# A decoder layer on one core: the attention branch's product for the prompt alone, weight splits in program order, and another order of the cache tiles

## The chip, the cores and the metric

One core of one Trainium2 chip runs the whole kernel. The metric is the device time in microseconds, the median of several runs; lower is better.

## What is computed

One decoder layer with shared weights for two groups of tokens: a prompt of 512 tokens and 32 sampled tokens (8 sequences of 4, each with 4096 past tokens in a paged cache). D is 1024, there are 8 heads of 64, everything is fp32. Cut to what matters here:

```
h  = rms_norm(x) * (1 + sc_m) + sh_m
u, q, k, v, g_a, g_b = split(h @ w_in)
a  = pool_mixer(u) @ w_branch_pool
o  = attend(q, k, v) @ w_branch_attn        # prompt: block-sparse; sampled: over the cache
m  = sigmoid(g_a) * a + sigmoid(g_b) * o
x  = x + gt_m * (m @ w_out)
h2 = rms_norm(x) * (1 + sc_f) + sh_f
x  = x + gt_f * ((silu(conv3(h2 @ w_up_gate)) * (h2 @ w_up_val)) @ w_down)
```

The six vectors sh_m, sc_m, gt_m, sh_f, sc_f, gt_f (modulations 0 to 5) are products of the tokens' conditions with w_ada.

## The kernel before

**Layout.** The 544 columns (512 of the prompt, then 32 sampled) lie feature-major and are worked in two halves of 272 columns (`BOTH`, `HALF`). A product in fp32 is made of three fp32r products, `mm3` (line 458): weight hi by input hi, hi by lo, lo by hi. So every weight tile is split in two on chip: ScalarE copies it to `hi` (line 182) and VectorE subtracts to get `lo` (line 179); `split` (line 184) writes both.

**Weights.** `granule_plan` (line 54) lists the 512 KB granules in the order of use: q, k, v, u, then ga, ga, bp four times (gate a and the pool branch), gb eight times, ba four times (the attention branch), wo eight times, then the feed-forward part: 44 granules ahead of the latter. `W.pump` (line 214) loads them on SP's queue into a ring of three staging tiles `st` (some at the start in pairs, `pair`). `W.get` (line 239) hands out a split granule and has the next one split at once (`conv`, line 225), into rings of two `hi` and two `lo`; wo's granules get tiles of their own (`woh`, `wol`). A scheduler of the framework then sets each engine's order of instructions from its own estimates, so a split may stand elsewhere in ScalarE's or VectorE's order than where it is written, unless it is pinned. `pin` (`keep_in_program_order`) ties an instruction behind the instruction written before it on its engine.

**Two streams.** `dense1` (line 483) is the dense work up to wo. `kv_stream` (line 1006) works the paged cache for the sampled tokens: 64 key tiles of 1 MB (products `qk`), two softmaxes of 4 sequences each (`soft`, line 1054), 64 value tiles (`pv`, 8 per sequence), and the modulations 2 to 5 from w_ada (`mod`, `one`). Its tiles come on POOL's queue into a ring of six buffers `kv`, in the order of `kv_order` (line 1335): 32 key tiles, 4 more, 32 value tiles, the other 28 key tiles, modulations 4 and 5 (4 tiles each), 32 value tiles, modulations 2 and 3 (8 tiles). PE takes them in visits of four tiles (`RUN`) which a loop (after line 1297) puts between pieces of `dense1` by its own estimate of PE's clock and of each tile's landing; a stream can also wait for a named state (`need`). PE, ScalarE and VectorE each work their instructions in the resulting order.

**The end of the two streams.** After the last gate product `dense1` waits for `oTs` (line 900), the sampled attention of all eight sequences; `finish` (line 1012) makes it: it masks a sequence's `pv` result, and its `rest` transposes it (`oT`) ahead of the next visit and reduces it into `oTs`. Then come the O products (line 907 on, two halves of 272 columns), the split of the merged m (`mh`, `ml`), the need for modulations 2 and 4, and wo (line 977 on): eight products over the first half of the columns, eight over the second. After each, `residual` (line 940) adds x (loaded again from `xT`) and ScalarE squares the sum (`sq`).

Of the kernel before, what the change touches and what calls it, by code (L numbers as in the profile page):

```python
# [73 lines left out]
def body(ctx, tc, I, O):  # L74
# [46 lines left out]
    V, A = nc.vector, nc.scalar  # L121

# [82 lines left out]
    class Weights:  # L205
# [19 lines left out]
        def conv(self, i):  # L225
            if i >= len(self.jobs) or self.jobs[i][1] or i in self.done:
                return
            self.pump()
            st = self.tiles.pop(i)
            if i in self.hooks:  # L230
                self.hooks.pop(i)(st)
            hi, lo = self.place.pop(i)() if i in self.place else (wsh.next(), wsl.next())
            split(hi, lo, st)
            self.done[i] = (hi, lo)
            self.ready[i] = max(PE.now, self.landed.pop(i)) + SPLIT_US
            self.held -= 1
            self.pump()
# [26 lines left out]
    csT = consts.tile([128, KD, 32], F32, name="csT")  # L264
# [4 lines left out]
    cst = consts.tile([128, NCONST], F32, name="cst")  # L269
    par = consts.tile([128, NPAR], F32, name="par")  # L270
# [4 lines left out]
    ones = consts.tile([128, 1], F32, name="ones")  # L275
    V.memset(ones, 1.0)

    pin = tc.keep_in_program_order
# [40 lines left out]
    class Stream:  # L319
# [7 lines left out]
        def pump(self):  # L327
            while self.issued < len(self.items) and self.issued < self.at + NKV:
# [32 lines left out]
                self.landed[self.issued] = Q.move(1.0, POOL_US.get(kind, 1.0))  # L361
# [25 lines left out]
    modT = consts.tile([128, 6, 8, 9], F32, name="modT")  # L387
# [95 lines left out]
    def dense1():  # L483
# [90 lines left out]
        def heads_sampled(name, got):  # L574
# [4 lines left out]
            if name == "q":  # L579

                qa = consts.tile([128, 4, 2, 32], F32, name="qall")
# [12 lines left out]
            else:  # L594
                hs = consts.tile([128, 4, NS], F32, name=name + "sT")
# [155 lines left out]
        def weigh(i, f):  # L751
# [8 lines left out]
            if i == 3:  # L760
                of = slot([128, T])
                act(of[:, 0:S], o)
                attn.append(of)
# [88 lines left out]
        Tt = []  # L852
        def gate(f, sig):
# [8 lines left out]
        for f0 in range(0, 8, 2):  # L862
# [6 lines left out]
            for f in (f0, f0 + 1):  # L869
                yield from gate(f, sig_a)  # L870
                if f == 0:
# [4 lines left out]
            for f in (f0, f0 + 1):  # L876
# [10 lines left out]
        sg = {}  # L887

        def sig_b(f, ps):
            sg[f] = slot([128, T])  # L890
            for o, (a, b) in zip(ps, BOTH):
                act(sg[f][:, a:b], o, AF.Sigmoid)
        for f in range(8):
            yield from gate(f, sig_b)
        ohl = []
        for of in attn:
            oh, ol = slot([128, T], F32R), slot([128, T], F32R)
            split(oh[:, 0:S], ol[:, 0:S], of[:, 0:S])
# [5 lines left out]
        yield ("lat", 2.0)  # L904
        for f0 in range(0, 8, 2):
            ba = W.get()
# [9 lines left out]
        ohl.clear()  # L916


        mh, ml = [slot([128, T], F32R) for _ in range(8)], [slot([128, T], F32R) for _ in range(8)]
        for f in range(8):  # L920
            split(mh[f], ml[f], Tt[f])
# [53 lines left out]
        for a, b in BOTH:  # L975
            pr, sq = mm([128, HALF], "ss"), []
# [29 lines left out]
    def kv_stream():  # L1006
        fin, Ls, PTs, own_p, stats, pvs = [], {0: [], 1: []}, {}, {}, {}, {}
# [4 lines left out]
        def finish(n, pv):  # L1012
# [4 lines left out]
            def rest():  # L1017
# [4 lines left out]
                if n == NSEQ - 1:  # L1022
                    state["oTs"] = True
            fin.append(rest)

        def kstep(g, c):
# [13 lines left out]
            if c % 4 == 3:  # L1040
# [6 lines left out]
                Ls[g].append(l)  # L1047
            if c == NPG - 1:
# [92 lines left out]


# [8 lines left out]
        while todo:  # L1151
            kind, a = todo[0]
            if kind == "done":
# [4 lines left out]
            while n < min(RUN, len(todo)) and todo[n][0] in ("k", "v", "m"):  # L1158
                if todo[n][0] == "v":
                    yield ("need", "PT%d" % (todo[n][1][0] // 4))  # L1160
                    yield ("need", "vs")
# [3 lines left out]
            while fin:  # L1165
                fin.pop(0)()
                yield ("x", 0.45)
# [12 lines left out]
            PE.end()  # L1180
            del todo[:n]
# [153 lines left out]
def kv_order():  # L1335
# [3 lines left out]
    return k[0] + k[1][:4] + v[:32] + k[1][4:] + [("one", 4), ("one", 5)] + v[32:] + [("mod", 1)]  # L1339
# [129 lines left out]
```

## Time and profile before

| what | value |
|---|---|
| runs | 981.67, 982.39, 984.0 us; median 982.39 |
| profiled execution | 982.47 us, its span 980.7 us, granted TensorE clock 0.982 of full speed |
| busy, share of the span | PE 95%, VectorE 48%, ScalarE 33%, POOL 14% |
| moved | 231.77 MB: 151.00 MB on POOL's queue, 79.48 MB on SP's |

PE is TensorE's matmuls; DVE is VectorE, ACT is ScalarE. Matmuls are pipelined and their ends are modelled, so a row's own duration is not its cost: the cost of one in a row of equal products is the distance between starts. In the profile each value tile shows eight `pv` records (in the order listings below, four products). Rows in square brackets give the idle time before an instruction and what ended it.

### The profile page before, as it was taken

The numbers are of one execution on the slowest core, as the hardware profiler recorded it, in microseconds if no ns is written. First come the engines' busy times: TensorE is split into PE (matmuls) and PEld (weight loads), VectorE is DVE, ScalarE is ACT, GpSimd is POOL, SyncE is SP. The second block draws the span as 40 slices with busy tenths as digits, with TensorE's granted clock in tenths as the row PEclk, the third lists the DMA queues.
The fourth block names the chain that finished last, engine by engine and source line by source line (L and its number), as shares of the span: only waits on it lengthen the run. The fifth ranks groups of instructions, "written<-read, shape, count | busy, mean of one in ns | idle before, by whom it ended". The sixth has DMA issues, their size and how long they took to land.

```text
span 980.7 us, 20374 instructions
## 1 busy us (share of the span) xinstructions
PE 931.1 (95%) x8724; PEld 807.0 (82%) x8724; DVE 475.1 (48%) x1155; ACT 323.3 (33%) x645; POOL 138.1 (14%) x153
## 2 busy tenths in 40 slices
PE   4999998799899999998699999999999999999998
PEld 2567776555589998874279999999999999999998
DVE  5673526766413234222157656554454546444643
ACT  4352426633312226312034544332322323123210
POOL 0133333033423322334200000000000000000000
PEclk9999999999999999999799999999999999999999
DMA  9799999399989999899976102222222222222332
GB/s 359 271 397 415 402 422 378 146 358 370 367 335 415 399 416 402 342 420 418 422 290 222 64 1 87 88 89 89 98 91 87 86 87 86 87 87 87 94 98 81
DMA packets 45354, 231.77 MB, mean 236 GB/s; under 512 B 5136, under 2 KB 6672, under 8 KB 25808
## 3 DMA queue, kind: packets, MB, share of 16 engines
q0 software_dynamic: 20736, 151.00, 38.0%
q1 hardware_dynamic: 24528, 79.48, 23.1%
q8 instruction: 68, 1.11, 0.5%
q14 instruction: 22, 0.18, 0.1%
HBM read 225.52 MB, written 4.94 MB: 235 GB/s over the span
## 4 chain that ended last, share of the span: by engine, by line
PE 82%; DVE 8%; DMA 4%; ACT 3%; issue 2%; POOL 0%; ACTq 0%; POOLq 0%; DVEq 0%
PE up L162 26%; PE dn L162 13%; PE gate L162 10%; PE qkv L162 7%; PE qk L162 5%; PE pv L162 5%; PE wo L162 4%; PE A L162 3%; DMA kv<-in_v,vidx 3%; PE mod L162 2%; DVE s L179 2%; ACT s L182 2%; PE paO L162 1%; PE paS L162 1%; DMA st<-in_wpack 1%
## 5 line engine op out<-in xcount | busy, mean ns | idle before, releaser
L162 PE MATMUL up<-s,hi 128*128 128x272 f32 x1408 | 237.5, 289 | 1.1 <-ACT hi L182 0.6
L179 DVE TENSOR_TENSOR lo<-st,hi 128x1024 fp32r<-128x1024 f32 x101 | 123.7, 1224 | 215.3 <-ACT hi L182 214.9
L182 ACT ACTIVATE hi<-st 128x1024 fp32r<-128x1024 f32 x101 | 107.1, 1060 | 313.7 <-PE up L162 106.8
L162 PEld LDWEIGHTS up<-s,hi 128*128 128x128 f32 x1408 | 199.6, 188 | 2.7 <-ACT hi L182 0.9
L162 PE MATMUL up<-s,lo 128*128 128x272 f32 x704 | 147.6, 287 | 0.5 <-DVE lo L179 0.5
L162 PE MATMUL dn<-s,hi 128*128 128x272 f32 x704 | 116.9, 287 | 0.0
L162 PEld LDWEIGHTS up<-s,lo 128*128 128x128 f32 x704 | 111.2, 188 | 0.7 <-DVE lo L179 0.7
L162 PEld LDWEIGHTS dn<-s,hi 128*128 128x128 f32 x704 | 99.3, 188 | 0.0
L162 PE MATMUL gate<-s,hi 128*128 128x272 f32 x512 | 89.0, 295 | 0.0
L339 POOL DMA_INDIRECT kv<-in_kT,kidx x64 | 64.1, 1001 | 175.6 <-PE qk L162 105.3
L343 POOL DMA_INDIRECT kv<-in_v,vidx x64 | 63.8, 997 | 144.5 <-PE pv L162 111.6
L162 PEld LDWEIGHTS gate<-s,hi 128*128 128x128 f32 x512 | 73.3, 191 | 6.3 <-issue 6.0
L162 PE MATMUL pv<-kv,spots 128*32 128x512 f32 x512 | 66.2, 647 | 11.1 <-DMA kv<-in_v,vidx 9.6
L162 PE MATMUL dn<-s,lo 128*128 128x272 f32 x352 | 73.4, 288 | 0.0
L162 PE MATMUL qkv<-hi,s 128*128 128x512 f32 x192 | 68.1, 415 | 3.5 <-ACT s L182 3.3
L182 ACT ACTIVATE s<-s 128x544 f32<-128x544 f32 (+4 forms) x76 | 46.7, 639 | 73.3 <-DVE s L1217 37.5
L162 PE MATMUL qk<-kv,qblk 128*32 128x128 f32 x2048 | 59.3, 273 | 0.0
L162 PEld LDWEIGHTS qk<-kv,qblk 128*32 128x32 f32 x2048 | 54.9, 110 | 3.9 <-issue 2.2
L162 PEld LDWEIGHTS pv<-kv,spots 128*32 128x32 f32 x512 | 17.7, 141 | 48.6 <-issue 24.0
L162 PEld LDWEIGHTS qkv<-hi,s 128*128 128x128 f32 x192 | 36.5, 191 | 23.5 <-issue 10.1
L162 PEld LDWEIGHTS dn<-s,lo 128*128 128x128 f32 x352 | 55.3, 188 | 0.0
L162 PE MATMUL gate<-s,lo 128*128 128x272 f32 x256 | 53.5, 291 | 0.0
(198 smaller groups left out, 1249.2 us busy)
## 6 DMA issues: line engine op xcount, KB each, us to landing
st<-in_wpack SPq DMA_DIRECT2D x108, 512.0 KB, 3.5
kv<-in_wada POOLq DMA_DIRECT2D x16, 1024.0 KB, 10.9
kv<-in_wada SPq DMA_DIRECT2D x5, 1024.0 KB, 15.2
s<-in_xT SPq DMA_DIRECT2D x16, 272.0 KB, 4.9
pair<-in_wpack SPq DMA_DIRECT2D x6, 512.0 KB, 8.0
m<-in_wada SPq DMA_DIRECT2D x3, 1024.0 KB, 15.2
out_y<-s SPq DMA_DIRECT2D x7, 272.0 KB, 2.0
kv<-in_kT,kidx POOLq DMA_INDIRECT x64, 9.8
```

The lines of the kernel that those rows point to most:

```text
L162: return self.add(nc.tensor.matmul(out, lhsT, rhs, **kw))
L179: V.tensor_tensor(out, a, b, op)
L182: A.activation(out, x, func, **kw)
L339: pin(nc.gpsimd.indirect_dma_start(out=kt, out_offset=None, in_=krows, in_offset=bass.IndirectOffsetOnAxis(ap=kidx[:, i:i + 1], axis=0)))
L343: pin(nc.gpsimd.indirect_dma_start(out=kt, out_offset=None, in_=vrows, in_offset=bass.IndirectOffsetOnAxis(ap=vidx[:, i:i + 1], axis=0)))
```

## The change

- The plan takes gb, gb, ba four times, so each branch product follows its two gates. The O product is made for the prompt's 512 columns in one piece and no longer needs `oTs`.
- The sampled tokens' branch is a visit of its own, `branch`, after the last value tile: the four ba granules are loaded a second time, unsplit, on POOL's queue (items `w1`); 32 small products with 32-column weights (`late`), two copies, eight transposes, two reductions, the gating, eight splits of 32 columns. wo's second half needs it (state `ms`).
- `kv_order`: eight key tiles instead of four ahead of the first values; modulations 2 and 3 ahead of the second 32 values, 4 and 5 behind the branch.
- Each weight split is pinned, on ScalarE and on VectorE.
- The transposes of a sequence's output are issued after the next visit instead of before it; the copy of the eighth of the second group's key tiles (`put`) is put off to the next value visit.
- Several constant tiles become parts of one tile `keep`; `w_pool_group` and `state_poolT` are loaded with the v instead of the k granules.

```diff
@@ granule_plan
-    for f in range(0, 8, 2):
-        plan += [("ga", f), ("ga", f + 1), ("bp", f // 2)]
-    plan += [("gb", f) for f in range(8)] + [("ba", f) for f in range(4)]
+    for gate, branch in (("ga", "bp"), ("gb", "ba")):
+        for f in range(0, 8, 2):
+            plan += [(gate, f), (gate, f + 1), (branch, f // 2)]
@@ Weights.conv
-            split(hi, lo, st)
+            pin(A.activation(hi, st, AF.Copy))
+            pin(V.tensor_tensor(lo, st, hi.bitcast(F32), OP.subtract))
@@ Stream.pump
+                elif kind == "w1":
+                    pin(nc.gpsimd.dma_start(kt[:, 0:1024], I["wpack"][gi[a]]))
@@ sampled inputs
-            if name == "k":
+            if name == "v":
                 wpg = slot([128, 4, 128])
...
@@ dense1, behind the gates
-                for o, (a, b) in zip(pa, BOTH):
-                    tt(sg[f][:, a:b], o, sg[f][:, a:b], OP.mult)
-                Tt.append(sg[f])
+                tp = slot([128, S])
+                tt(tp[:, 0:HALF], pa[0], sg[f][:, 0:HALF], OP.mult)
+                tt(tp[:, HALF:S], pa[1][:, 0:S - HALF], sg[f][:, HALF:S], OP.mult)
+                tt(Ts[:, f], pa[1][:, S - HALF:HALF], sg[f][:, S:T], OP.mult)
+                Tt.append(tp)
...
-        yield ("need", "oTs")
-        for k in range(4):
-            split(ohl[k][0][:, S:T], ohl[k][1][:, S:T], oTs[:, k])
...
         for f0 in range(0, 8, 2):
+            sg = {}
...
+            for f in (f0, f0 + 1):
+                yield from gate(f, sig_b)
             ba = W.get()
             for f in (f0, f0 + 1):
-                po = [mm([128, HALF], "O") for _ in range(2)]
+                po = mm([128, S], "O")
                 for k in range(4):
                     c = slice(((f % 2) * 4 + k) * 128, ((f % 2) * 4 + k + 1) * 128)
-                    mm3(po, ba[0][:, c], ba[1][:, c], ohl[k][0], ohl[k][1], BOTH, k == 0, k == 3)
+                    mm3([po], ba[0][:, c], ba[1][:, c], ohl[k][0], ohl[k][1], ((0, S),), k == 0, k == 3)
                     yield 0.65
-                for o, (a, b) in zip(po, BOTH):
-                    tt(sg[f][:, a:b], o, sg[f][:, a:b], OP.mult)
+                tt(sg[f], po, sg[f], OP.mult)
                 tt(Tt[f], Tt[f], sg[f], OP.add)
@@ wo
         for a, b in BOTH:
+            if a:
+                yield ("need", "ms")
@@ kv_stream
+        def branch():
+            while fin:
+                fin.pop(0)()
+            KV.pump()
+            yield ("lat", 1.5)
+            pb = [mm([128, 4, 128], "late") for _ in range(2)]
+            yield ("at", KV.landed[KV.at + 3])
+            PE.begin()
+            for f in range(8):
+                if f % 2 == 0:
+                    wt = KV.get("w1")
+                for k in range(4):
+                    PE.matmul(pb[f // 4][32 * k:32 * k + 32, f % 4], oTs[:, k], wt[:, ((f % 2) * 4 + k) * 128:((f % 2) * 4 + k + 1) * 128],
+                              start=True, stop=True)
+                if f % 2 == 1:
+                    KV.next()
+            PE.end()
+            yield ("lat", 2.0)
...
+            yield ("need", "sgs")
+            tt(om, om, state["sgs"], OP.mult)
+            tt(om, om, state["Ts"], OP.add)
+            yield ("need", "m")
+            for f in range(8):
+                split(state["m"][0][f][:, S:T], state["m"][1][f][:, S:T], om[:, f])
+            state["ms"] = True
...
-            while fin:
-                fin.pop(0)()
-                yield ("x", 0.45)
+            ends = list(fin)
+            fin.clear()
...
             PE.end()
+            for x in ends:
+                x()
@@ kv_order
-    return k[0] + k[1][:4] + v[:32] + k[1][4:] + [("one", 4), ("one", 5)] + v[32:] + [("mod", 1)]
+    return k[0] + k[1][:8] + v[:32] + k[1][8:] + [("mod", 1)] + v[32:] + [("branch", 0), ("one", 4), ("one", 5)]
```

PE, the end of the value tiles, before (`gate` is a gb product, `pv` a value product, `oT` the transposes of a sequence's output, `O` the branch product); listings leave out where nothing new stands:

```order
L162 MATMUL gate_4801<-s_127,lo 128x272
L162 MATMUL pv_4838<-kv,spots 32x512 x16
L162 MATMUL pv_4838<-s_1470,s_4456 32x128 x4
L166 MATMUL oT_4916<-cst,s_4914 128x128 x4
L162 MATMUL pv_4922<-kv,spots 32x512 x32
L162 MATMUL pv_4922<-s_1470,s_4456 32x128 x4
L166 MATMUL oT_4969<-cst,s_4967 128x128 x4
L162 MATMUL O_4986<-s_4874,hi 128x272
```

And now, at the last visit:

```order
L163 MATMUL pv_4924<-kv,spots 32x512 x16
L163 MATMUL pv_4924<-s_1464,s_4403 32x128 x4
L163 MATMUL gate_5000<-s_120,hi 128x272
...
L167 MATMUL oT_5052<-keep,s_5050 128x128 x4
...
L163 MATMUL late_5070<-kv,oTs 32x128 x16
L163 MATMUL late_5071<-kv,oTs 32x128 x16
L163 MATMUL gate_5000<-s_123,hi 128x272
...
L163 MATMUL O_5127<-s_4211,hi 128x512
...
L163 MATMUL mod_5243<-kv,keep 32x512 x16
L163 MATMUL mod_5264<-keep,s_5262 128x64 x4
L163 MATMUL wo_5294<-s_5174,hi 128x272
```

Behind the last value visit stand 24 gate products, the branch, the last 24 of 96 O products and modulation 4; the 72 others and the gates stand between the visits, where before no dense product was left for the last twelve tiles.

ScalarE, the weights of wo (`woh`), m's split (`s`), and the squares behind wo's products (`sq`), before:

```order
L182 ACTIVATE woh_5543<-st 128x1024
L182 ACTIVATE s_5276<-s_3682 128x544
L182 ACTIVATE s_5277<-s_3941 128x544
L182 ACTIVATE woh_5407<-st 128x1024
L182 ACTIVATE s_5278<-s_4099 128x544
L182 ACTIVATE hi<-st 128x1024
L182 ACTIVATE sq_5372<-s_5305 128x272
L182 ACTIVATE sq_5405<-s_5307 128x272
L182 ACTIVATE sq_5438<-s_5309 128x272
L182 ACTIVATE woh_5508<-st 128x1024
```

And now:

```order
L183 ACTIVATE s_5262<-mod_5243 128x512
L235 ACTIVATE woh_5289<-st 128x1024
L183 ACTIVATE sq_5320<-s_5208 128x272
L235 ACTIVATE woh_5322<-st 128x1024
L183 ACTIVATE sq_5353<-s_5210 128x272
L235 ACTIVATE woh_5355<-st 128x1024
L183 ACTIVATE sq_5386<-s_5212 128x272
L235 ACTIVATE woh_5388<-st 128x1024
```

Splits and squares now take turns, and none of the seven splits stands ahead of modulation 4's copy.

VectorE at the start, the first granule's `lo`, the modulation's row (`gsm`) and the first of h, before:

```order
L179 TENSOR_TENSOR modT<-mod_221,par 128x2x18
L179 TENSOR_TENSOR lo<-pair_110,hi 128x1024
L542 SCALAR_TENSOR_TENSOR gsm<-modT,par 128x18
L179 TENSOR_TENSOR xsT<-s_86,s_138 128x32
L179 TENSOR_TENSOR xsT<-s_87,s_138 128x32
L179 TENSOR_TENSOR h1s<-xsT,gsm 128x64
```

And now, from h's sampled columns on:

```order
L180 TENSOR_TENSOR s_124<-h1s,s_116 128x32
L180 TENSOR_TENSOR s_125<-h1s,s_117 128x32
L461 TENSOR_SCALAR s_229<-s_174,gsm,keep 128x512
L461 TENSOR_SCALAR s_233<-s_176,gsm,keep 128x512
L180 TENSOR_TENSOR s_124<-s_229,s_116 128x512
L180 TENSOR_TENSOR s_125<-s_233,s_117 128x512
L236 TENSOR_TENSOR lo<-pair_106,hi 128x1024
```

`lo` has moved from ahead of `gsm` to behind h's first two slices.

## Rows read from the trace of the kernel before

**Rows 1.** the page's head: span, then busy time, share and instructions of each engine.

```profile
span 980.7 us, 20374 instructions
PE 931.1 (95%) x8724; PEld 807.0 (82%) x8724; DVE 475.1 (48%) x1155; ACT 323.3 (33%) x645; POOL 138.1 (14%) x153
```

**Rows 2.** waits of PE: waiting line, releaser, us in total, times, longest.

```profile
PE pv L162 <- DMA kv<-in_v,vidx: 9.6, 9, 1.7
...
PE oT L166 <- DVE s L179: 1.7, 2, 0.9
...
PE wo L162 <- DVE s L179: 1.6, 1, 1.6
```

**Rows 3.** timeline of PE, 457 to 488: start, us, names, [idle before and releaser].

```profile
457.49 1.09 PE L162 MATMUL pv<-kv,spots 128*32 128x512 f32 x8
...
464.55 1.94 PE L162 MATMUL pv<-kv,spots 128*32 128x512 f32 x8 [1.73 <-DMA kv<-in_v,vidx]
...
485.35 1.09 PE L162 MATMUL pv<-kv,spots 128*32 128x512 f32 x8 [0.69 <-DMA kv<-in_v,vidx]
486.26 0.40 PE L162 MATMUL pv<-s,s 128*32 128x128 f32 x8
487.48 0.66 PE L166 MATMUL oT<-cst,s 128*128 128x128 f32 x4 [0.81 <-DVE s L179]
487.89 0.49 PE L162 MATMUL O<-s,hi 128*128 128x272 f32 x2
```

**Rows 4.** windows: length, PE, PEld, DVE, ACT, POOL busy, clock, DMA share, GB/s.

```profile
460.00:490.00 30.00, 19.37 (x123) 6.07 (x120) 5.43 (x12) 1.64 (x7) 8.39 (x12) 0.77 1.01 422
```

**Rows 5.** timeline of PE, 160 to 200: prompt attention, key visit, value visit.

```profile
160.24 0.86 PE L162 MATMUL paO<-s,s 128*64 128x128 f32 x4 [3.29 <-ACT s L182]
...
164.54 3.70 PE L162 MATMUL qk<-kv,qblk 128*32 128x128 f32 x128
...
196.21 3.67 PE L162 MATMUL pv<-kv,spots 128*32 128x512 f32 x32 [1.32 <-ACT s L182]
```

**Rows 6.** timeline of PE, modulations 2 and 3 and the start of wo.

```profile
492.75 3.64 PE L162 MATMUL mod<-kv,csT 128*32 128x512 f32 x32
...
508.35 0.66 PE L166 MATMUL mod<-cst,s 128*128 128x128 f32 x4 [0.72 <-ACT s L182]
...
520.79 0.41 PE L162 MATMUL wo<-s,hi 128*128 128x272 f32 x2
```

**Rows 7.** timeline of PE, gate products of 272 columns (records between are six).

```profile
410.85 0.66 PE L162 MATMUL gate<-s,hi 128*128 128x272 f32 x4
...
411.60 0.66 PE L162 MATMUL gate<-s,hi 128*128 128x272 f32 x4
```

**Rows 8.** the chain that ended last, a run of 512-column products: start, us, what.

```profile
81.41 7.66 PE qkv L162 x35
```

**Rows 9.** DMA issues: out<-in, queue, count, KB each, us from issue to landing.

```profile
kv<-in_wada POOLq DMA_DIRECT2D x16, 1024.0 KB, 10.9
```

**Rows 10.** timeline of DVE in wo: a split's lo, a residual.

```profile
536.67 1.22 DVE L179 TENSOR_TENSOR wol<-st,woh 128x1024 fp32r<-128x1024 f32 x1 [3.72 <-ACT woh L182]
...
541.35 0.50 DVE L943 SCALAR_TENSOR_TENSOR s<-wo,modT,s 128x272 f32<-128x272 f32 x1 [1.65 <-PE wo L162]
```

**Rows 11.** timeline of ACT in wo: a split's hi, a square.

```profile
535.58 1.06 ACT L182 ACTIVATE woh<-st 128x1024 fp32r<-128x1024 f32 x1 [2.12 <-DMA st<-in_wpack]
538.39 0.43 ACT L182 ACTIVATE sq<-s 128x272 f32<-128x272 f32 x1 [1.75 <-PE wo L162]
```

**Rows 12.** timeline of DVE at the start: the first lo, the modulation's row.

```profile
20.02 1.22 DVE L179 TENSOR_TENSOR lo<-pair,hi 128x1024 fp32r<-128x1024 f32 x1
21.16 0.17 DVE L542 SCALAR_TENSOR_TENSOR gsm<-modT,par 128x18 f32<-128x18 f32 x1
```

**Rows 13.** timeline of PE at the start: the first q product.

```profile
22.23 0.80 PE L162 MATMUL qkv<-hi,s 128*128 128x512 f32 x1 [3.31 <-ACT s L182]
```

**Rows 14.** a window in which DMA moved nothing.

```profile
185.00:195.00 10.00, 9.86 (x84) 7.32 (x82) 6.23 (x19) 7.67 (x20) 0.00 (x0) 1.00 0.00 1
```

More of the change, by code (lines that the diff above doesn't have):

```diff
@@ L121, in body @@
     V, A = nc.vector, nc.scalar
+    pin = tc.keep_in_program_order
     class Tensor:
@@ L263, in body @@
     nc.sync.dma_start(cT, I["cT"])
-    csT = consts.tile([128, KD, 32], F32, name="csT")
+    keep = consts.tile([128, NCONST + NPAR + 256 + 432 + 4 + 384], F32, name="keep")
+    cst, par = keep[:, 0:NCONST], keep[:, NCONST:NCONST + NPAR]
+    csT = keep[:, NCONST + NPAR:NCONST + NPAR + 256].rearrange("p (k m) -> p k m", k=KD)
+    modT = keep[:, NCONST + NPAR + 256:NCONST + NPAR + 688].rearrange("p (v f m) -> p v f m", v=6, f=8)
     V.memset(csT, 0.0)
@@ L268, in body @@
     act(warm, csT[:, 0, 0:1], AF.Sqrt, scale=0.0)
-    cst = consts.tile([128, NCONST], F32, name="cst")
-    par = consts.tile([128, NPAR], F32, name="par")
     ptb = consts.tile([128, 256], I32, name="ptb")
     xT = [slot([128, T]) for _ in range(KD)]
-    ones = consts.tile([128, 1], F32, name="ones")
+    small_end = NCONST + NPAR + 692
+    ones = keep[:, NCONST + NPAR + 688:NCONST + NPAR + 689]
     V.memset(ones, 1.0)
-    pin = tc.keep_in_program_order
     def in_order(ins):
@@ L360, in pump @@
                 self.tiles[self.issued] = kt
-                self.landed[self.issued] = Q.move(1.0, POOL_US.get(kind, 1.0))
+                self.landed[self.issued] = Q.move(0.5 if kind == "w1" else 1.0, POOL_US.get(kind, 1.0))
                 self.issued += 1
@@ L384, in body @@
             KV.items += [("one", (a, k)) for k in range(4)]
-    modT = consts.tile([128, 6, 8, 9], F32, name="modT")
+        elif kind == "branch":
+            KV.items += [("w1", ("ba", i)) for i in range(4)]
     def modulation(i):
@@ L579, in heads_sampled @@
             if name == "q":
-                qa = consts.tile([128, 4, 2, 32], F32, name="qall")
+                qa = keep[:, small_end:small_end + 256].rearrange("p (f g c) -> p f g c", f=4, g=2)
                 qb = consts.tile([128, 4, 4, 2, 32], F32, name="qblk")
@@ L594, in heads_sampled @@
             else:
-                hs = consts.tile([128, 4, NS], F32, name=name + "sT")
+                hs = keep[:, small_end + 256:small_end + 384].rearrange("p (f t) -> p f t", f=4)
                 V.tensor_copy(hs, ps)
@@ L760, in weigh @@
             if i == 3:
-                of = slot([128, T])
-                act(of[:, 0:S], o)
+                of = slot([128, S])
+                act(of, o)
                 attn.append(of)
@@ L852, in dense1 @@
         Tt = []
+        Ts = consts.tile([128, 8, NS], F32, name="Ts")
+        sgs = consts.tile([128, 8, NS], F32, name="sgs")
         def gate(f, sig):
@@ L886, in dense1 @@
         pool.clear()
[L887 to L894, printed above, removed]
         ohl = []
         for of in attn:
-            oh, ol = slot([128, T], F32R), slot([128, T], F32R)
-            split(oh[:, 0:S], ol[:, 0:S], of[:, 0:S])
+            oh, ol = slot([128, S], F32R), slot([128, S], F32R)
+            split(oh, ol, of)
@@ L899, in dense1, with sig_b @@
             ohl.append((oh, ol))
-        yield ("need", "oTs")
-        for k in range(4):
-            split(ohl[k][0][:, S:T], ohl[k][1][:, S:T], oTs[:, k])
         attn.clear()
-        yield ("lat", 2.0)
         for f0 in range(0, 8, 2):
+            sg = {}
+            def sig_b(f, ps):
+                sg[f] = slot([128, S])
+                act(sg[f][:, 0:HALF], ps[0], AF.Sigmoid)
+                act(sg[f][:, HALF:S], ps[1][:, 0:S - HALF], AF.Sigmoid)
+                act(sgs[:, f], ps[1][:, S - HALF:HALF], AF.Sigmoid)
@@ L912, in dense1 @@
                     yield 0.65
-                for o, (a, b) in zip(po, BOTH):
-                    tt(sg[f][:, a:b], o, sg[f][:, a:b], OP.mult)
+                tt(sg[f], po, sg[f], OP.mult)
                 tt(Tt[f], Tt[f], sg[f], OP.add)
         ohl.clear()
+        state["Ts"], state["sgs"] = Ts, sgs
         mh, ml = [slot([128, T], F32R) for _ in range(8)], [slot([128, T], F32R) for _ in range(8)]
         for f in range(8):
-            split(mh[f], ml[f], Tt[f])
+            split(mh[f][:, 0:S], ml[f][:, 0:S], Tt[f])
@@ L922, in dense1 @@
+        state["m"] = (mh, ml)
         Tt.clear()
@@ L1006, in kv_stream @@
     def kv_stream():
+        puts = []
         fin, Ls, PTs, own_p, stats, pvs = [], {0: [], 1: []}, {}, {}, {}, {}
@@ L1047, in kstep @@
                 Ls[g].append(l)
+            if c % 4 == 3:
+                if (g, c) == (1, 7):
+                    puts.append(put)
+                else:
+                    put()
             if c == NPG - 1:
@@ L1140, in vstep @@
                     del PTs[g], own_p[g]
+        def branch():
[16 more added lines that the diff above has]
+            yield ("lat", 2.0)
+            om = sm([128, 8, NS], tag="hs", bufs=2)
+            for h in range(2):
+                ob = slot([128, 4, 128])
+                act(ob, pb[h])
+                ps = mm([128, 4, 128], "late")
+                for f in range(4):
+                    PE.transpose(ps[:, f], ob[:, f], ident)
+                V.tensor_reduce(om[:, 4 * h:4 * h + 4], ps.rearrange("p f (j t) -> p f t j", j=4), AX.X, OP.add)
+            yield ("need", "sgs")
[5 more added lines that the diff above has]
+            state["ms"] = True
         todo = []
@@ L1152, in kv_stream @@
             kind, a = todo[0]
+            if kind == "branch":
+                todo.pop(0)
+                yield from branch()
+                continue
             if kind == "done":
@@ L1160, in kv_stream @@
                     yield ("need", "PT%d" % (todo[n][1][0] // 4))
+                    while puts:
+                        puts.pop(0)()
                     yield ("need", "vs")
```

6 lines of the change are left out of this document (2 added, 4 removed).

## The prediction

> **What bounds the kernel now.** I read the page's first lines, then PE's waits, PE's timeline in the stretch with the largest wait, and the windows over it. The span is 980.7 us, of which PE is busy 931.1 [rows 1], so there are about 50 us that PE could save without less work. The feed-forward part is not where they are: the largest wait, and the one this change touches, is that of the sampled value products for their cache tiles, 9.6 us in nine waits [rows 2]. The timeline shows it from 457.49, where the last gate product is done, to 487.89, where the O products begin [rows 3]: the only work left for PE in between is twelve value tiles, and each comes late. The windows say why: the DMA engines are full (share 1.01) at 422 GB/s, and PE's granted clock falls to a mean of 0.77 [rows 4], while a visit's eight products keep their 1.09 to 1.10 us. So transfers set the pace there, and the O products, which need no more transfers than their own weights, stand behind the sampled attention of all eight sequences. The profiled execution took 982.47 us (980.7 and 1.8 around it), 0.08 over the median of the three runs; the sum is made against 982.47.
>
> **The prompt's O products go into that stretch.** It lasts 487.89 − 457.49 = 30.4 us. Work in it: twelve tiles at 3.67 / 4 = 0.92 us [rows 5] are 11.0, two products of the new tokens' own values 0.8 and two sets of transposes 1.0 [rows 3], 12.8 in all. PE is without work for 17.6 us, and O products now fill it: **−17.6**. That holds only if the last value tile also lands earlier; otherwise PE runs out of O products and waits again. Its landing: 485.35 before [rows 3]. Four key tiles leave the stretch between (see the hole, below): 4.2 MB at 0.42 MB per us [rows 4], −10 us; three branch granules of 0.5 MB come in, +3.7; so about 479. PE's arrival at it: 485.35, less the 16.9 us idle before it, plus 72 O products of the new size (15.8 us), less 24 gate products that the order now puts behind it (3.0), less the key visit (3.6), plus the modulation that is moved ahead of it (two visits of 3.64 and 1.4 of transposes [rows 6], 8.7 us, for 4.0 that go out), is 482.4. PE comes last by some 3 us: the two are nearly balanced, and this is where the sum is weakest. If the tile landed at 485 as before, 4.5 us of the gain would be gone.
>
> **O on 512 columns.** 192 products of 272 columns become 96 of 512. Six of 272 take 411.60 − 410.85 = 0.75 us, 0.125 each [rows 7]; 35 of 512 take 7.66, 0.219 each [rows 8]. 24.0 becomes 21.0: **−3.0**.
>
> **The sampled tokens' branch.** It adds 32 small products, eight transposes, two ScalarE copies, and on VectorE two reductions and two products, then eight splits of 32 columns on both. The small products have the shape of the key products (32-column weights, 128 columns); a key visit of four tiles holds 64 of these and takes 3.70 us [rows 5], 0.058 each, so 1.9. The transposes are two sets of four, 0.6 each, as in 0.66 for the old ones [rows 6]. **+3.1**. Its vector work lies beside O products and the wo products of the first column half; only the second half needs it. Four loads of 0.5 MB on POOL's queue come twice now, 5 us of transfer.
>
> **Modulation behind the branch.** The first of the two single modulations now stands between the last O product and wo, and its four 1 MB tiles can only be issued as the last value tiles free their buffers. After the last value tile 2.1 MB of branch weights and 4.2 MB come through one queue: 6.3 / 0.42 = 15 us, so it lands at 494 at the earliest, or later if wo's weights take a share; a modulation tile took 10.9 us from issue to landing [rows 9]. PE gets there at 482.4 + 1.1 + 3.0 of gates + 5.3 of O products + 3.1 of branch = 494.9. Bounds: nothing, and 5 us if wo's granules take a quarter of the bandwidth. I take **+1.5**, nearer to the balance.
>
> **Splits kept in program order.** Each of the 44 granules ahead of the feed-forward part, and those within it, gets its hi (ScalarE) and lo (VectorE) behind the instruction written before it. In the feed-forward part the order hardly changes. In wo it does: before, the splits ran ahead of the squares; now split f+1 stands behind the square of product f−1. After a product ends come the residual 0.50, the square 0.43, hi 1.06 and lo 1.22 [rows 10, 11], with handovers some 3.5 us, where a product of 24 times 0.125 lasts 3.0. A wait of 0.5 gives the next one 0.5 of slack, so I count every second of six: 1.5; the 1.6 us that wo's first product waited for VectorE [rows 2] may go, but the prompt's eight splits remain in front of it. **+1.0**, bounds −1.6 and +4. At the start the first lo stood ahead of the modulation's rows on VectorE (at 20.02, 1.22 us long [rows 12]) and now comes behind h's splits; the first q product, at 22.23 [rows 13], needs hi, which moves likewise behind two rows of 0.8. **+1.0**, bounds 0 and +3. In the second softmax the splits stand among the exponentials: **+0.5**, bounds −0.5 and +1.5. Behind those waits stands the whole dense stream, since PE takes its products in order.
>
> **An eighth group of keys before the first values.** One more key visit, 3.70 us, stands before the first value visit and thus in the prompt's attention, where PE waits for ScalarE (3.29 at 160.24, 1.32 at 196.21 [rows 5]); four buffers are freed in time, so four value tiles load while DMA moved nothing (share 0.00 for 10 us [rows 14]). PE could save 3.6 at most; an extra visit in front of the softmax could also delay it by as much as it takes. Bounds −4 and +1, **−2.0**.
>
> **Costed at nothing.** The merged constant tiles, the later loads of two small inputs (no wait of PE names them) and the transposes behind the next visit: these last took two waits, 1.7 us in all [rows 2], both within the stretch counted above. The xT loads in front of wo's last weights wait for the last O evictions; wo's fifth granule, the first behind them, is wanted 12 us after wo's start. Without that cover it would cost up to 3.
>
> Sum: −17.6 − 3.0 + 3.1 + 1.5 + 1.0 + 1.0 + 0.5 − 2.0 = −15.5, and 982.47 − 15.5 = **967.0 us**.
>
> **The Trainium skill at one place.** Into the stretch of the value tiles 422 GB/s came out of HBM [rows 4], and my landing time of 479 uses 0.42 MB per us. The Trainium skill, "DMA: Bandwidth & Descriptors", section "Where 436 GB/s comes from", says that for HBM to SBUF the limit is about 358 GB/s per core. By that, an estimate, the 32 MB from the first to the last value tile of the second half would take 89 us and not 76, and the gain would mostly go; the trace disagrees with 422, and the measurement decides.
>
> **The rivals.** (a) *The tail stays bound by transfers.* For it: the DMA share is 1.01 up to 490, and the ledger is balanced to 3 us; against it: the ten empty microseconds [rows 14], which the freed buffers can use. If none of those are used, the last value tile lands at 485 to 489, PE waits 3 to 6 us, and the single modulation lands that much later: 970 to 976. (b) *Slower: the pinned splits become PE's waits.* The place is the dense stream from q to wo: a split that ran as soon as its granule landed now stands behind a late ScalarE or VectorE row, of the prompt's attention or an eviction that itself waits for PE. The gain counted is 15.5; over 44 granules the point that decides is 0.35 us of wait per granule on top of what I counted. At 0.5 each the time is 967 + 22 = 989. Against it: waits on hi or lo are hardly in PE's list, wo gives 0.25 per granule at the worst place, and the gates' granule lasts 6 us against 2.3 for its split. For it: in the prompt's attention PE already waits for ScalarE's queue [rows 5]. The Trainium skill, "TensorE: Matmul & The Clock Gate", section "Architectural detail: the array is 16× 32×32, not 1× 128×128", states that ScalarE and VectorE work their queues strictly first in, first out; that speaks for this rival, and the trace agrees in that the modulation's row stood behind lo [rows 12]. (c) *More is gained:* the hole is used in full, the last tile lands at 476, no wait before wo, and the key visit costs nothing: 967 − 1.6 − 1.5 − 2.5 and the start's 1.0 give 960, at the bounds 957. (d) *The order changes but the time does not:* the order shows the O products among the visits, but if both (a) and a third of (b) come, 976 + 7 is again 982.
>
> **How the numbers follow.** The forecast with its small terms (961 to 970) gets 0.55, (a) 0.20, (c) 0.13, (b) 0.08, (d) 0.04. The range for 8 in 10 takes in the forecast, (a) and most of (c), with its upper end at the fringe of (d): 957 to 980. About 0.2%, 2 us, is what a measurement can tell from no change. Faster has the forecast, (a) and (c): 0.88; same (d): 0.04; slower (b): 0.08.
>
> **What would show it.** Right: value visits separated by O products without DMA waits, a granted clock at 1.0 in place of 0.77, the last value tile landing at 477 to 482, wo starting at 495 to 500 (520.79 before [rows 6]), the feed-forward part of the same length. Wrong: PE waits on hi or lo of a microsecond or more in the q, u or gate products (b); value waits and a wait for the modulation's tiles before wo, with wo at 503 or later (a); a wait of over 0.7 us in front of most of wo's products in its first half (my bound for the splits).

## The result, and the profile after

| | before | changed |
|---|---|---|
| runs | 981.67, 984.0, 982.39, 983.49 | 965.38, 966.08, 967.72, 968.57 |
| median, us | 982.94 | 966.9 |
| profiled execution, its span | 982.47, 980.7 | 965.38, 963.6 |

The ratio is 0.9838, 95% interval 0.9815 to 0.986: 16.0 us shorter. The forecast was 967.0 us, 957 to 980, faster with 0.88. The sum came out almost exactly; the experiments show that its parts were understood worse than that suggests, and that their errors nearly cancel.

Where the time went, by the starts and ends of PE's groups in the two profiles, in us:

| | before | changed |
|---|---|---|
| first q, first u product | 22.23, 146.3 | 23.13, 148.3 |
| first value product | 196.21 | 198.81 |
| first gate product | 268.3 | 268.3 |
| end of the last value tile's products | 486.4 | 476.9 |
| first wo product | 520.79 | 496.26 |
| first product of the feed-forward part | 575.3 | 556.8 |
| last product | 976.5 | 959.4 |

The page's head of the changed kernel, which answers to [rows 1]:

```profile
span 963.6 us, 20327 instructions
PE 924.6 (96%) x8700; PEld 802.7 (83%) x8700; DVE 479.8 (50%) x1163; ACT 323.4 (34%) x659; POOL 141.3 (15%) x157
```

PE is busy 6.5 us less, and idle 10.6 us less. Its waits, against [rows 2]:

```profile
PE mod L163 <- ACT s L183: 2.6, 2, 2.1
...
PE wo L163 <- DVE wol L236: 2.2, 2, 1.5
...
PE pv L163 <- DMA kv<-in_v,vidx: 0.4, 1, 0.4
```

The 9.6 us of waits for value tiles are 0.4 now, and the transposes' 1.7 us are gone. Windows over the last value tiles, against [rows 4] (columns as there):

```profile
450.00:460.00 10.00, 10.00 (x73) 7.17 (x66) 3.24 (x4) 1.77 (x5) 3.75 (x4) 1.00 1.01 419
460.00:470.00 10.00, 10.00 (x84) 7.41 (x83) 3.21 (x4) 0.99 (x1) 3.40 (x4) 1.00 1.02 418
470.00:480.00 10.00, 10.00 (x93) 7.37 (x93) 2.61 (x3) 1.69 (x4) 2.11 (x4) 1.00 0.97 340
```

PE is never idle, its granted clock is 1.00 where it was 0.77, and the DMA engines are full to 470: PE and the transfers end within a few us of each other, PE last. PE's timeline from the last visit to wo, against [rows 3] and [rows 6]:

```profile
473.24 3.67 PE L163 MATMUL pv<-kv,spots 128*32 128x512 f32 x32
476.73 0.40 PE L163 MATMUL pv<-s,s 128*32 128x128 f32 x8
...
479.96 1.95 PE L163 MATMUL late<-kv,oTs 128*32 128x128 f32 x64
...
485.01 1.15 PE L167 MATMUL late<-keep,s 128*128 128x128 f32 x8
...
489.32 3.93 PE L163 MATMUL mod<-kv,keep 128*32 128x512 f32 x32
495.34 1.11 PE L163 MATMUL mod<-keep,s 128*128 128x64 f32 x8 [2.09 <-ACT s L183]
496.26 0.49 PE L163 MATMUL wo<-s,hi 128*128 128x272 f32 x2
```

By the distance of starts (from 479.96 and 485.01 to the next products, at 481.85 and 485.91) the branch costs 1.9 + 0.9 = 2.8 us. In front of wo PE waits 2.09 us, not for the modulation's tiles but for ScalarE. ScalarE's and then VectorE's timeline there:

```profile
493.23 0.35 ACT L183 ACTIVATE s<-hs 128x32 fp32r<-128x32 f32 x2 [3.71 <-DVE hs L180]
...
494.72 0.57 ACT L183 ACTIVATE s<-mod 128x512 f32<-128x512 f32 x1
```

```profile
493.12 0.68 DVE L180 TENSOR_TENSOR s<-s,s 128x512 fp32r<-128x512 f32 x1
497.91 0.18 DVE L1277 COPY gs<-stc 128x16 f32<-128x16 f32 x1 [4.12 <-DMA stc<-in_state_convT]
498.00 0.68 DVE L180 TENSOR_TENSOR s<-s,s 128x512 fp32r<-128x512 f32 x1
```

The modulation's copy stands behind the branch's small splits (`hs`). And a copy of the feed-forward part stands among m's last splits on VectorE and waits 4.12 us for a load that came late through the full queues.

### The profile page after: what moved, and what is told of

Read it like the earlier page. It is cut to its first block, busy times and chain, and to the rows that moved or that the text cites. A ratio compares the mean times of both kernels' runs of the same rounds, so it can differ in the third digit from the quotient of the medians.

```text
span 963.6 us, 20327 instructions
## 1 busy us (share of the span) xinstructions
PE 924.6 (96%) x8700; PEld 802.7 (83%) x8700; DVE 479.8 (50%) x1163; ACT 323.4 (34%) x659; POOL 141.3 (15%) x157
## 4 chain that ended last, share of the span: by engine, by line
PE 54%; DVE 3%; DMA 2%; ACT 0%; SPq 0%; issue 0%; ACTq 0%
PE up L163 26%; PE dn L163 14%; PE gate L163 5%; PE pv L163 3%; PE wo L163 3%; PE O L163 2%; DMA stc<-in_state_convT 1%; DVE xn L180 1%; DMA st<-in_wpack 1%; DVE s L980 1%; PE mod L163 0%; SPq L302 0%; PE ss L163 0%; PE PT L167 0%; DVE s L967 0%; DVE s L180 0%
## 5 line engine op out<-in xcount | busy, mean ns | idle before, releaser
L163 PE MATMUL pv<-kv,spots 128*32 128x512 f32 x512 | 60.3, 600 | 1.2 <-ACT s L183 0.8
L180 DVE TENSOR_TENSOR s<-s,s 128x512 f32<-128x512 f32 (+4 forms) x72 | 48.8, 698 | 13.0 <-ACT s L183 12.5
```

Source lines behind the costliest of these rows:

```text
L163: return self.add(nc.tensor.matmul(out, lhsT, rhs, **kw))
L180: V.tensor_tensor(out, a, b, op)
```

## The experiments

They ran on three chips; each time is compared with the kernel before on the same chip. Where a label says keys, tiles ahead of the first values are meant.

**Four key tiles ahead instead of eight.**

```diff
-    return k[0] + k[1][:8] + v[:32] + k[1][8:] + [("mod", 1)] + v[32:] + ...
+    return k[0] + k[1][:4] + v[:32] + k[1][4:] + [("mod", 1)] + v[32:] + ...
-                if (g, c) == (1, 7):
+                if (g, c) == (9, 9):
```

> The changed kernel with four key tiles instead of eight ahead of the first values (and without the put-off copy, which only the eighth group needs). Theory (the extra key visit ran in PE's waits of the prompt's attention and filled the DMA's empty stretch): the first value product comes 0.6 us earlier or less, not 3.7, so the time is 3 us longer, 969 to 971, and DMA's empty 10 us between 185 and 195 come back. Rival (the visit is only moved, DMA is not short): within 1 us of the changed kernel's 966.9.

Measured: 987.5 us, ratio to before 1.0052 (1.0035 to 1.0069): 20 us longer than the changed kernel, the whole gain and more. Both readings had it at some 3 us at most. The first value product came at 202.3, 3.5 us later than with the extra visit. The windows from 150 to 205 of before, of the changed kernel and of this one:

```profile
150.00:205.00 55.00, 46.52 (x521) 33.97 (x514) 37.24 (x139) 31.45 (x100) 10.35 (x11) 0.97 0.67 255
```

```profile
150.00:205.00 55.00, 49.42 (x701) 37.56 (x689) 36.56 (x136) 34.10 (x107) 16.91 (x16) 0.97 0.81 320
```

```profile
150.00:205.00 55.00, 45.67 (x564) 34.29 (x567) 34.44 (x131) 32.11 (x101) 9.02 (x10) 0.91 0.58 229
```

320 less 229 GB/s over 55 us are 5.0 MB, 12 us of transfers at 0.42 MB per us, and from 300 to the last value tile the DMA engines are full in all three (mean share 0.99 to 1.00). So what is not moved here can hardly be caught up later: the last value tile's products end at 493.6, 16.7 us later than in the changed kernel. In the same window PE's granted clock is 0.91 where the changed kernel has 0.97, so a part of the extra visit's worth may be clock; that was not taken apart. The end of PE's timeline in e2_keys4:

```profile
489.97 3.67 PE L163 MATMUL pv<-kv,spots 128*32 128x512 f32 x32
493.46 0.40 PE L163 MATMUL pv<-s,s 128*32 128x128 f32 x8
498.69 1.11 PE L167 MATMUL oT<-keep,s 128*128 128x128 f32 x4 [4.83 <-DVE s L180]
...
511.27 1.74 PE L163 MATMUL mod<-kv,keep 128*32 128x512 f32 x8 [3.81 <-DMA kv<-in_wada]
```

All gate and O products are done (the last starts at 489.6) when PE takes up the last visit, so nothing stands beside what follows: wo starts at 518.5, 24.9 us behind the last value tile's products. In the changed kernel it is 19.4 us, with 24 gate and 24 O products among them. The granted clock over these stretches is 0.72 and 1.00.

**The same with O behind the sampled attention again.** The plan goes back to eight gb and then four ba granules, and O waits for the last sequence.

```diff
...
+        for f in range(8):
+            yield from gate(f, sig_b)
+        yield ("need", "oTs")
         for f0 in range(0, 8, 2):
-            for f in (f0, f0 + 1):
-                yield from gate(f, sig_b)
             ba = W.get()
...
```

> The same as e2_keys4, but with the O products waiting for the sampled attention of all sequences again (all gb gates first, then the ba granules), O still on 512 columns for the prompt only. Against e2_keys4 it undoes one thing. Theory (the gain is PE's empty time between the last value tiles, 17.6 us less the 2.1 us wait that came in at the modulation): 14 to 17 us longer than e2_keys4, some 984 to 986, with waits of value products for their tiles and the granted clock under 0.9 there. Rival (the gain comes from the narrower O and the order of the tiles): under 5 us longer than e2_keys4.

Measured: 990.06 us, ratio 1.0069 (1.0046 to 1.0093): only 2.6 us longer than e2_keys4, where 14 to 17 were expected. The waits for value tiles are back (10.9 us in eleven times), the last value tile's products end at 490.8. So with transfers this late the O products only fill time in which PE then waits elsewhere. This run lacks both the fill and the early keys and keeps the rest of the change: the rest costs 7 us against the kernel before (3 us of it by the first u product, at 149.4 for 146.3, and 3.3 between wo and the feed-forward part).

**The state's copy pinned**, in the changed kernel and in e2_keys4.

```diff
-                    V.tensor_copy(gs[:, :, 0:2], stc[:, f]...)
+                    (pin if f == 0 else (lambda x: x))(V.tensor_copy(gs[:, :, 0:2], stc[:, f]...))
```

> The changed kernel with one more pin: the first copy of the convolution's state (the first feed-forward tile's) stays behind what is written before it on VectorE, so it no longer stands ahead of the last splits of m. Theory (VectorE stood 4.12 us on the state's load from 493.80 on, and wo's first two products then waited 1.6 us for VectorE): 1 to 2 us shorter, 965 to 966, wo's waits for VectorE under 1 us in its first two products. Rival (PE's 2.1 us wait for ScalarE at the modulation comes from the same place): 3 to 4 us shorter. Rival (the splits of m wait anyway): no shorter.

> e2_keys4 (four key tiles ahead of the first values) with that pin on the state's copy, which in e2_keys4 stood 3.2 us ahead of the masking of the last value result, and so ahead of the last transposes, the branch and the modulation. Theory (most of e2_keys4's 20 us are the late last value tile, 493 in place of 476): 3 to 5 us shorter than e2_keys4's 987.5, 983 to 985. Rival (the misplaced copy is the cause): back to 970.

Measured: e5_copy 968.96, ratio 0.984 (0.981 to 0.987), no gain; e2c_keys4_copy 985.54, ratio 1.0013 (0.9989 to 1.0037), by the ratios 3.8 us better than e2_keys4, as its theory had it. The misplaced copy is the cause neither of the changed kernel's last waits nor of most of e2_keys4's 20 us. In e5_copy the copy's wait is gone, and wo's products wait for their granules' splits instead:

```profile
505.61 0.52 PE L163 MATMUL wo<-s,woh 128*128 128x272 f32 x2 [0.72 <-ACT woh L235]
506.87 0.39 PE L163 MATMUL wo<-s,wol 128*128 128x272 f32 x1 [0.73 <-DVE wol L236]
514.45 0.52 PE L163 MATMUL wo<-s,woh 128*128 128x272 f32 x2 [1.12 <-ACT woh L235]
```

**Splits not pinned.** Once for granules 0 to 43, once for 0 to 35. (There are 48 granules ahead of the feed-forward part; the prediction and the first expectation miscounted them as 44, so wo's last four stayed pinned in the first run too; in the second all eight did.)

```diff
-            pin(A.activation(hi, st, AF.Copy))
-            pin(V.tensor_tensor(lo, st, hi.bitcast(F32), OP.subtract))
+            hold = (lambda x: x) if i < 44 else pin
+            hold(A.activation(hi, st, AF.Copy))
+            hold(V.tensor_tensor(lo, st, hi.bitcast(F32), OP.subtract))
```

> The changed kernel without the pins on the splits of the 44 granules ahead of the feed-forward part; there the order of the splits is free again. Theory (pins cost PE 2 us up to the first u product and 1.5 us in wo): 2 to 4 us shorter, 963 to 965. Rival 1 (pins pay elsewhere, as between the first value and the first gate product, where the changed kernel was 2.6 us shorter): 0 to 3 us longer, and that stretch 72 us long again, not 69.5. Rival 2 (slower pins): over 10 us shorter.

> The changed kernel with the splits of the first 36 granules unpinned (q to the third pair of gb), those of the last ba and of wo pinned. Theory (e1_unpinned lost its time at the end, where wo's second granule, still in transfer, stood ahead of m's splits on ScalarE and PE waited 7.4 us; at the start it gained 2.8 us by the first u product): 962 to 965, first u product at 145 to 146. Rival (the free order costs in the gates too): 968 or more.

Measured: e1_unpinned 977.2 (970 to 979), ratio 0.9954 (0.9939 to 0.997), 10 us longer than the changed kernel; e1d_unpinned36 965.26, ratio 0.9802 (0.9769 to 0.9834), the same as the changed kernel within the intervals. So the pins that pay are among granules 36 to 43, the last two gates, two of ba and four of wo. The profiled execution of e1_unpinned is the fastest of its six, 970.23, 4.9 us longer than the changed kernel's; what the other five (975 to 979) lose beyond that no trace shows. Its ScalarE's timeline, and then PE's:

```profile
495.38 1.06 ACT L236 ACTIVATE woh<-st 128x1024 fp32r<-128x1024 f32 x1 [7.62 <-DMA st<-in_wpack]
496.35 2.17 ACT L183 ACTIVATE s<-s 128x512 fp32r<-128x512 f32 x4
```

```profile
501.89 1.97 PE L163 MATMUL mod<-keep,s 128*128 128x64 f32 x8 [7.42 <-ACT s L183]
```

Left free, a split whose granule is still in transfer stands ahead of m's splits and holds ScalarE for 7.62 us; wo starts at 503.6. In e1d_unpinned36 the first u product comes at 146.7 and the first gate product at 267.0, both over 1 us earlier than in the changed kernel, and yet the last value tile's products end at 476.9, as there. The lead is lost right behind the first gate product: in the 6.7 us from there PE's granted clock is 0.66, where the changed kernel has 1.00, and the next value visit starts at 271.6, in the changed kernel at 270.9. In e1_unpinned, with its full clock there, PE keeps the lead: first gate product 266.2, end of the last value tile's products 474.0, 2.9 us earlier than in the changed kernel. So in these traces the pins cost some 2 us up to there.

**No fill, but early keys.** e1d_unpinned36 with O waiting as in e3_wait.

> e1d_unpinned36 with the O products waiting for all sequences' sampled attention: eight key groups ahead, but no fill. Together with e2_keys4 and e3_wait it makes the square of fill and early keys. Theory (the fill is worth what PE does between the last tiles: 72 O products, 15.8 us, less 24 gate products that stand behind the last tile otherwise, 3.0, less the wait at the modulation, 2): 9 to 13 us longer than e1d_unpinned36, while the last value product ends at 474 to 480 in both. Rival (as between e2_keys4 and e3_wait): 2 to 3 us longer.

Measured: 973.55, ratio 0.9893 (0.9862 to 0.9924), 8.3 us longer than e1d_unpinned36, between the rival and the theory. PE waits 6.9 us for value tiles, and the last one's products end at 472.4. Now the square is full, in median us:

| | four key tiles ahead | eight |
|---|---|---|
| O waits for all sequences | 990.06 | 973.55 (36 granules unpinned) |
| O among the value visits | 987.5 | 966.9 (965.26 with 36 unpinned) |

Early keys are worth 16.5 us without the fill and 20.6 with it; the fill 2.6, hardly clear of the noise, and 8.3. The two columns were not measured on the same chip; by the ratios early keys are worth 17 and 21. Each needs the other for its full worth.

**O in two halves of 256 columns.**

```diff
-                po = mm([128, S], "O")
+                po = [mm([128, 256], "O") for _ in range(2)]
-                    mm3([po], ..., ((0, S),), k == 0, k == 3)
+                    mm3(po, ..., ((0, 256), (256, S)), k == 0, k == 3)
```

> The changed kernel with each O product of 512 columns as two of 256. It takes only the width apart. Theory (a product's price is a start and its columns: 0.125 for 272, 0.219 for 512, so 0.118 for 256 by the line between them): 192 times 0.118 less 96 times 0.219 = 1.6 us longer, 968 to 969, if PE is the bound where they stand. Rival (PE there waits for transfers anyway): no longer, within 0.5 us in the span of the profile.

Measured: 969.41, ratio 0.9867 (0.9848 to 0.9887). The time says little, since O already starts 3.7 us later than in the changed kernel. The starts say more. First the changed kernel's, then these:

```profile
398.88 0.63 PE L163 MATMUL O<-s,hi 128*128 128x512 f32 x2
...
399.58 0.62 PE L163 MATMUL O<-s,hi 128*128 128x512 f32 x2
```

```profile
402.55 0.64 PE L163 MATMUL O<-s,hi 128*128 128x256 f32 x4
...
403.27 0.64 PE L163 MATMUL O<-s,hi 128*128 128x256 f32 x4
```

Three products of 512 take 0.70 us, 0.23 each, six of 256 take 0.72, 0.12 each: 22.4 against 23.0 us in all. The width is worth 0.6 us.

**Transposes ahead of the next visit.**

```diff
-            ends = list(fin)
-            fin.clear()
+            while fin:
+                fin.pop(0)()
+                yield ("x", 0.45)
+            ends = []
```

> The changed kernel with the transposes of a sequence's output ahead of the next visit again, as before. Theory (they cost a wait only where nothing else stood between: 1.7 us before, all of it in the stretch that is now filled): within 1 us of the changed kernel's 966.9. Rival (the transposes wait for VectorE ahead of every second visit): 2 us longer or more.

Measured: 1003.73, ratio 0.9913 (0.9891 to 0.9936), on a chip where the kernel before took 1012.56. The changed kernel did not run on that chip, so the verdict stays open; the profile is on the rival's side, with waits of transposes of which the changed kernel has none:

```profile
PE oT L167 <- DVE s L180: 7.0, 4, 2.5
...
PE oT L167 <- issue: 4.0, 2, 2.4
```

**A modulation in the empty stretch.** If transfers bound everything up to the last value tile, a tile moved where DMA is idle is free.

```diff
-    return k[0] + k[1][:8] + v[:32] + ... + v[32:] + [("branch", 0), ("one", 4), ("one", 5)]
+    return k[0] + k[1][:8] + [("one", 4)] + v[:32] + ... + v[32:] + [("branch", 0), ("one", 5)]
```

> The changed kernel with modulation 4's four tiles between the eighth key group and the first values, in the stretch where DMA still moved nothing (195 to 205), instead of behind the branch. Theory (transfers bound the kernel up to the last value tile; these four tiles fill 10 of the 13 us that are empty between 150 and 205, and the visit runs in PE's waits for ScalarE): the last value product ends within 3 us of 477 as now, the modulation's visit, 3.6 us, and its wait for ScalarE, 2.1, are gone in front of wo, and the time is 4 to 6 us shorter, 961 to 963. Rival (the first values come later by the visit and all behind them too): within 1 us.

> As e9b_one4_hole, with modulation 5's four tiles there too; nothing but the branch stands behind the last value tile. By the same theory only 3 of its 10 us of transfers find an empty DMA, the rest delays the values: the last value product ends 5 to 8 us later than in e9b_one4_hole, 4.7 us of modulation are gone from wo, and the time is within 2 us of e9b_one4_hole. Rival (PE alone is the bound): 4 us shorter than e9b_one4_hole.

> e9b_one4_hole once more, because the chip of that run was slower with every kernel (the kernel before took 1012.6 us there, and a key visit 4.8 us in place of 3.65), so that its time does not stand beside the changed kernel's 966.9. Theory as there: on a chip where the kernel before takes 982 to 984, 955 to 963, a ratio of 0.97 to 0.98; the modulation's visit and its wait are gone in front of wo and the last value product ends within 3 us of 477. Rival (the gain there came from that chip's slow key visits): a ratio of 0.982 to 0.986, as the changed kernel has.

Measured: e9b_one4_hole 985.71, ratio 0.9727 (0.9705 to 0.9749), and e9a_ones_hole, with modulation 5 there too, 985.34, ratio 0.9737 (0.9711 to 0.9762), both on the slower chip; the two are the same, as expected. The repetition on a chip where the kernel before took 982.34: **960.06 us, ratio 0.9769 (0.9749 to 0.9788)**, clear of the changed kernel's 0.9815 to 0.986. Its window, and the end of its timeline:

```profile
150.00:205.00 55.00, 49.85 (x697) 36.50 (x692) 34.17 (x122) 31.48 (x97) 15.63 (x18) 0.94 0.95 380
```

```profile
479.33 0.40 PE L163 MATMUL pv<-s,s 128*32 128x128 f32 x8
...
494.08 3.64 PE L163 MATMUL mod<-kv,keep 128*32 128x512 f32 x32
498.43 1.10 PE L163 MATMUL mod<-keep,s 128*128 128x64 f32 x8 [0.72 <-ACT s L183]
```

In the window 3.3 MB more are moved than in the changed kernel, and the last value tile's products end at 479.5, 2.6 us later than there and not 10. Modulation 5 now stands where 4 stood, with a wait of 0.72 us for ScalarE instead of 2.09, no modulation stands within wo, and the feed-forward part starts at 551.6, 5.1 us earlier.

## Why the prediction was right, and where it was not

- **The sum.** That it came out to within 1 us is in part luck. Fill and key visit stand in it with 19.6 us; taken back together (e3_wait) they are worth 23. The other terms come to +4.1; in e3_wait the rest costs 7. The two errors nearly cancel, and between fill and key visit the gain lies the other way round than forecast.
- **The fill, −17.6.** As foreseen, PE has no idle time left among the last value tiles. But taken back alone it is worth 8.3 us (e3d_wait_keys8): with early keys PE waits less for value tiles even without it, 6.9 us. The term also took a visit's eight products as 1.09 to 1.10 us throughout; in [rows 3] one tile takes 1.94, and PE's waits in those 30.4 us add up to 11.3. And the sentence beside it, that 4.5 us would be lost if the last tile landed as before, and rival (a) with 970 to 976, were far off: with that landing not improved, e2_keys4 took 987.5. The step that failed there is the price of a late last tile. It counted PE's wait ahead of the tile, 3 to 6 us. In e2_keys4 PE's list has no wait for a value tile: PE works all dense products first and takes up the last visit at 489.97, close to the rival's 489. The loss stands behind it, where transposes, branch and modulation have nothing beside them.
- **The key visit, −2.0.** Its work for PE came out at about −3: the first value product comes 2.6 us later, 2.0 of it lost by the first u product already, with 3.65 us of work more done. Its worth is elsewhere, 16.5 us without the fill and 20.6 with it: the tiles' 12 us of transfers in the stretch that was empty [rows 14]. The prediction used that in the landing time (−10, about 479; the last visit's products ran from 473.24 to 476.9), but put the gain under the fill alone.
- **O, −3.0.** It was about −1.6: 0.23 each, not 0.219. The price came from one count in the chain [rows 8], and the distance of starts is the better source.
- **The branch, +3.1.** Measured 2.8, 1.9 for the products as forecast and 0.9 for the transposes, not 1.2.
- **Modulation behind the branch, +1.5.** 2.09 us of wait, for ScalarE and not for tiles. The two single modulations were also mis-sized: a visit takes 3.6 us like the others and not 2.0, which is some 5 us of the difference between PE's forecast arrival at the last tile, 482.4, and the measured one, 476 (three tiles of 0.92 behind 473.24). The tile came earlier than the forecast's 479 too, since PE starts on it without a wait; so the balance held although both times were off. The second one within wo makes 4.7 us of the 6.0 by which the stretch from wo to the feed-forward part is longer.
- **Pins.** wo: 1.3 us beside that modulation, for +1.0. Start: +0.9 at the first q product for +1.0, and +2.0 by the first u product. Rival (b), at 0.08, has the opposite sign: free splits at the end cost 10 us by the medians. The Trainium skill, "TensorE: Matmul & The Clock Gate", section "Architectural detail: the array is 16× 32×32, not 1× 128×128", has ScalarE and VectorE first in, first out. The 7.62 us row of e1_unpinned agrees, and it is the reason why the pins help: program order keeps a split that can't start yet from standing first.
- **Not foreseen:** from the first value to the first gate product it takes 69.5 us for 72.1. The granted clock goes with it. First the windows before and now (columns as in [rows 4]), then two of PE's waits before:

```profile
196.21:268.29 72.08, 65.27 (x568) 38.43 (x569) 40.19 (x132) 24.81 (x69) 26.41 (x26) 0.96 0.92 364
```

```profile
198.81:268.30 69.49, 63.24 (x564) 37.45 (x565) 40.80 (x133) 24.85 (x69) 26.12 (x26) 1.00 0.90 357
```

```profile
240.94 0.60 PE L162 MATMUL paO<-s,s 128*64 128x128 f32 x4 [1.97 <-ACT s L182]
...
266.73 2.15 PE L162 MATMUL pg<-s,s 128*128 128x272 f32 x4 [3.56 <-DVE s L179]
```

Before, the clock was at the lower of its two levels, 1.2 GHz, from 242.0 to 245.5, behind the first of these waits, and from 265.9, within the second, to 272.8. A value visit in the first stretch took 4.89 us and not 3.67. Now the waits at the same places are 1.18 and 2.34 us, and the clock stays at 2.4 GHz. In the other runs, the slower chip's left out, the stretch takes 69.1 to 69.5 us where its granted clock is 1.00 and 69.9 to 70.3 where it is 0.98 or 0.99, with pins and without, with four and with eight early tiles. So the clock accounts for the difference; which part of the change shortened the two waits stays open.
- **The feed-forward part** is 1.4 us longer (402.6 for 401.2), cause open.
- **The transfers' ceiling.** The windows show 418 to 420 GB/s for 70 us. The limit of about 358 from HBM in the Trainium skill, "DMA: Bandwidth & Descriptors", section "Where 436 GB/s comes from", which is there a stack's rate divided by its two cores, does not bind here, where one core runs.

## What to carry to other kernels

Where one queue of transfers bounds a long stretch, its idle time early on is the resource: fill PE's waits at the end only together with the transfer queue's empty stretches, and price a late last tile by all that stands behind it. A free scheduler may put a copy whose data is still in transfer at the head of an engine's queue; pin it behind work that others wait for. Look at the granted clock of a stretch before putting its time down to the order of instructions. Before believing a sum that came out right, undo its parts one at a time.

## What was not expected of the hardware

One of the three chips ran every kernel slower (before: 1012.56 us), with transfer rates of up to 420 GB/s as elsewhere, but longer key visits. The first one of e9b_one4_hole there:

```profile
68.02 4.13 PE L163 MATMUL qk<-kv,qblk 128*32 128x128 f32 x123
72.45 0.45 PE L163 MATMUL qk<-kv,qblk 128*32 128x128 f32 x5 [0.31 <-issue]
```

It takes 4.8 us to the next product, where the first key visit of the kernel before takes 3.6 (66.26 to 69.89), with waits in which the profile names nothing but PE's own issue. So a few us between runs on different chips say nothing; only the ratio to the kernel before on the same chip does, and even that can shift where one part, as the many small key products, is slower and another not.
